# Attention's probabilities turned by VectorE and a trip through DRAM, in a mixed retention and attention layer

## The chip, the cores and the metric

One Trainium2 chip, one of its cores. A core has TensorE (PE, matmuls), VectorE (DVE), ScalarE (ACT), GpSimd (POOL) and SyncE (SP, which here only issues transfers); every engine runs its own instructions in order. Work passes between engines through semaphores, and DMA queues move data between DRAM and the on-chip memories. The metric is the device time of one execution in microseconds (us), as the median of several runs.

## What is computed

A layer of a language model on 512 tokens and 16 meta tokens, all in float32: a feed-forward part, a mixer, a second feed-forward part. The change lies in the mixer's attention (8 heads of 128), of which the reference says, cut to what matters:

```python
def hybrid_mixer(u, pos, k_top, w_in, w_ret_out, w_att_out, w_mix_out):
    proj = u @ w_in
    rq, rk, rv, rg, aq, ak, av, iq, ik, iw, g_ret, g_att = jnp.split(proj, offs, axis=-1)
    yr = retention(rope(rq), rope(rk), rv)          # four heads, normalised
    yr = (jax.nn.silu(rg) * yr) @ w_ret_out
    ya = dsa_attention(rope(aq), rope(ak), av, rope(iq), rope(ik), iw, k_top) @ w_att_out
    merged = jax.nn.sigmoid(g_ret) * yr + jax.nn.sigmoid(g_att) * ya
    return merged @ w_mix_out
```

`dsa_attention` picks 128 keys for each query by an index score, adds the meta tokens, takes the softmax over the keys that are picked and sums their values with these probabilities. (The shapes and arguments are shortened here.)

## The kernel before

**Products.** Every float32 product is made of three products of a shorter type: each operand is split into a high and a low part (`split`: a copy by ACT, L117, and a subtraction by DVE, L118), and high by high, high by low and low by high are added in PSUM (`mm3`, L157). Weights come in by `load_w` on SP's queue into `raw` (2 buffers) and are split into `whi` and `wlo` (3 buffers each); the issue of the loads is in SP's order with everything else that SP transfers.

**Order.** PE's order is that of the program text. ACT and DVE follow the text inside blocks of `manual_schedule(engines=BUSY)`; elsewhere, in attention among it, a scheduler puts their instructions in order, and SP's and POOL's as well. PSUM tiles come from two pools: `sm_tile` (one bank) and `mm_tile` (two banks, few buffers), which a projection of k (`psak`), the last rows of the scores (`psS3`), the wide gates (`psgate`, `psga`) and the weighted sum (`psao`) share.

**Attention**, about 891 to 1070 us of the span. For each head h there is a period on PE:

- `scores(q, k)`: four blocks of 128 queries (L1964; j = 2, 1, 0, 3), each over the keys up to its own block, 144, 272, 400 and 528 with the meta tokens. DVE adds the bias of the choice and finds the row's greatest, ACT takes the exponential (L1972 and on), DVE scales the rows to a sum of one (L1975). The results are `prob[j]`, tiles `pj0` to `pj3`, queries along partitions and keys along the row.
- `proj_q`, `proj_k`: projections of the next head (`psaq`, `psak`), followed by `rope_swap`: two copies by ACT (L1291, L1292), a product with the cosine on DVE (L1293), a product with the sine on POOL (L1294), the sum on DVE (L1295), and the split into `aq` and `ak`.
- `transpose_p`: the weighted sum needs keys along partitions. PE turns `prob` in 13 squares of 128 and a piece of 16 (L1988, L1990), into four PSUM tiles `psPT`, one for each 128 keys; each is split into `pth` and `ptl`. `split_rows` puts the last 16 keys into `ptail`.
- `wide_gate`: a projection for one of the gates, in an `mm_tile`, then a sigmoid on ACT (its table is loaded anew, since the exponential has another). A gate of the first kind multiplies an accumulator on POOL; one of the second (`gate_a`) is stored to DRAM, `gd`, from SP (L2010).
- `weigh_v` (`weighted`, L1536 and L1537): twelve matmuls over 512, 400, 272 and 256 queries and one small one for the meta tokens, into `psao`, which is split into `vo[..][:, h, :]`, the operand of the output projection `psat`.

The last head has no further projections; two gates stand in their place. The values come from DRAM (`vst`): `split_values` turns four heads' values at once from `vraw` into the high and low parts that lie in `vo` itself, in the place of the head's later result; the second four heads are split after head 1, and `place_tails` brings their last rows at head 3.

**Two other places.** In retention's last head (p = 3), `norm_sums(p)` puts four small matmuls in the midst of the projection `psak` (at step 4 of its 8; `between` in `mm3`), which wait for DVE's `fold`; `norm_diag(p)` at step 7 goes on from POOL's result, and `norm_all(p)` at step 2 of the next projection. Before the second feed-forward part, `rstd_folded` takes a PSUM tile `psn` (L225 to L267) and the gate's first tiles `psg` follow, which ACT's copies of the token blocks (`hTok`, L2089) still hold.

Of the kernel before, what the change touches and what calls it, by code (L numbers as in the profile page):

```python
# [18 lines left out]
P = 128  # L19
# [62 lines left out]
def kernel(ctx: ExitStack, tc: tile.TileContext, x, meta, g1, wg1, wu1, wd1, gm,  # L82
# [225 lines left out]
    fs = dpool.tile([P, 4, S], F32, name="fs")  # L308
    fk = dpool.tile([2, P, T], F32, name="fk")
    gd = dpool.tile([2 * KD, P, S], F32, name="gd")  # L310

    def gap(p, n):

# [1083 lines left out]
    if True:  # L1397
# [243 lines left out]
        def steps_of(tiles_, runs):  # L1641
            return [(*t, r, 0) for t, r in zip(tiles_, runs)]
# [196 lines left out]
            n = 4 - (h == p)  # L1839
            more += queries_keys(h) + gates[:n] + outputs(h - 1, beside_outputs(h - 1)) + gates[n:]  # L1840
        more += steps_of(tiles("gr", w_in, OFF_GR + 2 * P, 2), [proj("psgate", REAL, (), last_0), proj("psgate", REAL, (), last_1)])
        more += steps_of(tiles("ak", w_in, OFF_AK, 1), [proj("psak", None, ((4, lambda: norm_sums(p)), (7, lambda: norm_diag(p))), last_2)])
        more += steps_of(tiles("aq", w_in, OFF_AQ, 1), [proj("psaq", REAL, ((2, lambda: norm_all(p)), (4, lambda: two_normed_parts(p, 0)), (6, lambda: two_normed_parts(p, 2))), last_3)])
        more += outputs(p, lambda i: pick(2 + (i == 0)))
        more += steps_of(tiles("gr4", w_in, OFF_GR + 4 * P, 1), [proj("psgate", REAL, (), first_kq.append)])
# [56 lines left out]
    def gate_a(ps):  # L1902
# [3 lines left out]
        nc.scalar.activation(t, ps, AF.Sigmoid)  # L1906
        return t

    with pool("ao") as ao:
        vo = [ao.tile([P, AH, S], F32R, tag=f"vo{i}", name="vo") for i in range(2)]  # L1910
        ao_parts = [(vo[0][:, c, :], vo[1][:, c, :]) for c in range(AH)]
        with pool("at") as at:
            tp.update(pool=at, bufs=7)
            cos, sin = rope_tables(1, at)
            gap(at, 32)
            prob = []
            for j in range(4):
                wj = min(P * (j + 2), T)
                pj = at.tile([P, wj], F32, tag=f"pj{j}", name=f"pj{j}")
                if j < 3:  # L1920
                    nc.gpsimd.memset(pj[:, NM + P * (j + 1) :], 0.0)
                prob.append(pj)
            gap(at, 48)
            tails(at, 64)
            gap(at, 16)
            cq, ck = (Cols(w_in, o_ + P, AH - 1, step=1) for o_ in (OFF_AQ, OFF_AK))
# [52 lines left out]
            def scores(q, k):  # L1979
                for j in (2, 1, 0, 3):  # L1980
                    score(j, q, k)()

            def transpose_p():
                parts = []
                for kb in range(4):
                    ps = sm_tile("psPT")
                    for j in range(max(kb - 1, 0), 4):
                        nc.tensor.transpose(ps[:, j * P : (j + 1) * P], prob[j][:, kb * P : (kb + 1) * P], ident)  # L1988
                    if kb == 3:
                        nc.tensor.transpose(ps[:NM, 0:P], prob[3][:, 4 * P : T], ident)  # L1990
                    n = S - KQ[kb]
                    ph = at.tile([P, wide(n)], F32R, tag=f"pth{kb}", name="pth")[:, :n]
                    pl = at.tile([P, wide(n)], F32R, tag=f"ptl{kb}", name="ptl")[:, :n]
                    if kb == 3:
                        split_rows(ps[:NM, P - NM : P], tp["p"][:, :NM], "hlh")
                    split(ps[:, KQ[kb] :], ph, pl)
                    parts.append((ph, pl))
                return parts
# [14 lines left out]
            with tc.manual_schedule(engines=BUSY):  # L2013
                w = gr.next()
                k, q = rope_k(first_k, nc.vector), rope_q(first_q, nc.vector)
                t, t5 = (at.tile([P, S], F32, tag="gate", name="gate", bufs=2) for _ in range(2))
                nc.scalar.activation(t, first_gate, AF.Sigmoid)
                gate_acc(4, t)
                ps = mm_tile("psgate")[:, :S]
                mm3([(ps, REAL)], w, xs, KD)  # L2020
                w = cq.next()
                nc.scalar.activation(t5, ps, AF.Sigmoid)
                gate_acc(5, t5)
                for to_one in [score(j, q, k) for j in (2, 1, 0, 3)]:
                    to_one()
                vs = split_values(raw, [v[:, :4, :] for v in vo])
                raw = fetch_values(5, vraw())
            for h in range(AH):
                more = h + 1 < AH
                if h:  # L2030
                    scores(q, k)
                if more:
                    q, k = proj_q(w if h == 0 else None), proj_k()
                else:
                    wide_gate(sm_tile("psga"))
                    wide_gate()
                pt = transpose_p()
                wide_gate()
                weigh_v(h, pt, vs[h])
                if h == 1:  # L2040
                    with tc.manual_schedule(engines=BUSY):
                        more_vs = split_values(raw, [v[:, 4:, :] for v in vo])
                if h == 3:
                    place_tails(5)
                    vs += more_vs

        vrs.close()

        mgs = ExitStack()
        mgp = mgs.enter_context(pool("mgp", 1, side="right"))  # L2050
# [30 lines left out]
    with pool("om") as ou:  # L2081
        tp.update(pool=ou, bufs=3)
        def to_tokens(blocks):
            for c, hc in blocks:
                ps = sm_tile("psht")
                for b in range(4):
                    nc.tensor.transpose(ps[:, b * P : (b + 1) * P], hc[:, b * P : (b + 1) * P], ident)
                for b in range(4):
                    nc.scalar.activation(hTok[b][:, c * P : (c + 1) * P], ps[:, b * P : (b + 1) * P], AF.Copy)  # L2089

        cols = Cols(w_mo, 0, KD)
        pend = []
        for c in range(KD):
            hc = ou.tile([P, S], F32, tag="hc", name="hc", bufs=4)
            nc.scalar.dma_start(hc, hd[c])
            w = cols.next()
            ps = sm_tile("psmo")
            mm3([(ps, slice(0, S))], w, lambda k: mg[k], KD)
            if len(pend) == 2:
                to_tokens(pend)  # L2100
                pend = []
# [12 lines left out]

        norm = rstd_folded(ssum3, D, R3, ou, lambda: sm_tile("psn"))
        raw0 = load_w(wg2[:, 0 : 2 * P], KD, 2 * P)
        ps0 = [sm_tile("psg") for _ in range(2)]
        for i in range(2):
            w = split_w(raw0[:, :, i * P : (i + 1) * P])
            mm3([(ps0[i], RS)], w, xs, KD)  # L2120
            if i == 0:
                last_tokens()
                next(norm)
        raw0 = load_w(wu2[:, 0 : 2 * P], KD, 2 * P)
        w = split_w(raw0[:, :, :P])
        for _ in norm:
            pass
# [224 lines left out]
```

## Time and profile before

| | |
|---|---|
| median of 3 runs | 1516.9 us (1516.48 to 1517.41) |
| the profiled execution | 1516.42 us, of which the span from the first instruction to the last 1514.6 us |
| granted TensorE clock, mean | 0.998 |
| PE busy 0 to 891 us (first part, retention, choice of keys) | 888.8 us |
| PE busy 891 to 1070 us (attention) | 178.75 of 179.0 us |
| DVE, ACT busy in the same stretch | 120.5 us, 121.4 us |
| POOL busy, share of the DMA engines in the same stretch | 26.0 us, 0.35 |
| PE busy 1070 to 1130 us (output projections) | 60.0 of 60.0 us |
| PE busy 1130 to 1514 us (second feed-forward part) | 376.6 of 384.0 us |

A row of the profile gives engine, line of the kernel, operation, what is written and read, the partitions by elements of both, and the number of instructions; in the views over time the start stands first, then the duration, and in brackets how long the engine had been idle and what ended it. Matmuls overlap, so that the distance between starts tells what one costs. A group's row has busy time and mean duration, then the idle time before its instructions and its releasers. In the view of DMA issues the last number is the median time from issue to landing.

### The profile page before, as it was taken

What the parts mean: (1) busy time and instruction counts of PE and PEld (TensorE: products, weight loads), DVE (VectorE), ACT (ScalarE), POOL (GpSimd) and SP (SyncE); (2) the same over time, 40 slices, a digit from 0 to 9 for tenths busy, and PEclk for the clock granted to TensorE, in tenths of its full rate; (3) what the DMA queues carried; (4) which work ended last, traced back from release to release, by engine and by line L of the source; (5) the groups of instructions that cost most, each with busy time, mean ns of one, the idle gap of its engine ahead of it and who ended that gap; (6) DMA issues with size and microseconds to landing.
All of it is one profiled execution on the core that took longest, in us unless ns stands there. A gap on an engine that the chain in (4) does not pass through costs nothing.

```text
span 1514.6 us, 23886 instructions
## 1 busy us (share of the span) xinstructions
PE 1504.1 (99%) x9748; PEld 1368.1 (90%) x9748; DVE 1100.9 (73%) x1710; ACT 727.5 (48%) x1134; POOL 103.5 (7%) x135
## 2 busy tenths in 40 slices
PE   9999999999999999999999999999999999999997
PEld 8999999999988888888888888998888899899996
DVE  5988586786886768678888887665455888586675
ACT  5555263454354444443333357666345445264453
POOL 1000000003101120000000131110001000000000
PEclk9999999999999999999999999999999999999999
DMA  4232323226554444232323242333443223233232
GB/s 169 65 120 88 118 88 111 90 92 209 195 164 161 168 147 146 87 122 87 122 73 98 90 131 77 88 90 105 146 139 119 84 84 112 84 112 112 84 125 84
DMA packets 151741, 173.48 MB, mean 115 GB/s; under 512 B 4944, under 2 KB 123240, under 8 KB 150992
## 3 DMA queue, kind: packets, MB, share of 16 engines
q1 hardware_dynamic: 142992, 151.58, 31.6%
q0 software_dynamic: 3808, 11.38, 2.0%
q10 hardware_dynamic: 4832, 9.00, 1.6%
q8 instruction: 76, 1.25, 0.3%
q14 instruction: 33, 0.27, 0.1%
HBM read 155.94 MB, written 16.01 MB: 114 GB/s over the span
## 4 chain that ended last, share of the span: by engine, by line
PE 98%; ACT 0%; DVE 0%; issue 0%; POOL 0%; POOLq 0%; ACTq 0%
PE psqX L157 14%; PE psd L157 8%; PE psd L2187 8%; PE psqY L157 7%; PE psrg L157 6%; PE psro L157 6%; PE psvX L1180 4%; PE psqZ L157 3%; PE psrk L157 3%; PE psu L157 3%; PE psrq L157 3%; PE psaq L157 3%; PE psga L157 3%; PE psat L157 3%; PE psmo L157 3%; PE psak L157 3%
## 5 line engine op out<-in xcount | busy, mean ns | idle before, releaser
L328 ACT ACTIVATE whi<-raw 128x1024 fp32r<-128x1024 f32 (+2 forms) x184 | 169.5, 924 | 128.7 <-PE psd L157 37.6
L329 DVE TENSOR_TENSOR wlo<-raw,whi 128x1024 fp32r<-128x1024 f32 (+2 forms) x184 | 198.4, 1083 | 40.5 <-ACT whi L328 40.3
L157 PE MATMUL psqX<-th,whi 128*128 128x264 f32 (+1 forms) x432 | 122.3, 283 | 0.0
L157 PE MATMUL psqX<-tl,whi 128*128 128x264 f32 (+1 forms) x432 | 122.3, 283 | 0.0
L157 PE MATMUL psqX<-th,wlo 128*128 128x264 f32 (+1 forms) x432 | 122.2, 283 | 0.0
L118 DVE TENSOR_TENSOR wlo<-raw,whi 128x1024 fp32r<-128x1024 f32 (+1 forms) x60 | 73.6, 1227 | 52.4 <-ACT whi L117 51.5
L328 ACT ACTIVATE whi<-wsum 128x1024 fp32r<-128x1024 f32 x72 | 76.3, 1060 | 70.6 <-PE psd L2187 22.0
L117 ACT ACTIVATE whi<-raw 128x1024 fp32r<-128x1024 f32 (+1 forms) x60 | 62.3, 1043 | 85.7 <-PE psat L157 26.6
L329 DVE TENSOR_TENSOR wlo<-wsum,whi 128x1024 fp32r<-128x1024 f32 x72 | 87.8, 1221 | 12.5 <-ACT whi L328 12.5
L157 PEld LDWEIGHTS psqX<-th,whi 128*128 128x128 f32 x432 | 82.1, 190 | 0.2 <-DVE g L544 0.2
L157 PEld LDWEIGHTS psqX<-th,wlo 128*128 128x128 f32 x432 | 82.0, 190 | 0.0
L157 PEld LDWEIGHTS psqX<-tl,whi 128*128 128x128 f32 x432 | 82.0, 190 | 0.0
L157 PE MATMUL psro<-vo,whi 128*128 128x512 f32 x256 | 78.8, 389 | 0.0
L157 PE MATMUL psd<-hl,whi 128*128 128x264 f32 x352 | 71.4, 284 | 0.0
L157 PE MATMUL psd<-hh,wlo 128*128 128x264 f32 x352 | 70.8, 283 | 0.0
L157 PE MATMUL psd<-hh,whi 128*128 128x264 f32 x352 | 70.6, 282 | 0.0
L2187 PE MATMUL psd<-wlo,hh 128*128 128x512 f32 (+1 forms) x182 | 69.2, 382 | 0.0
L2187 PE MATMUL psd<-whi,hh 128*128 128x512 f32 (+1 forms) x182 | 69.2, 382 | 0.0
L2187 PE MATMUL psd<-whi,hl 128*128 128x512 f32 (+1 forms) x182 | 69.2, 382 | 0.0
L157 PEld LDWEIGHTS psro<-vo,whi 128*128 128x128 f32 x256 | 48.1, 188 | 10.1 <-DVE vo L329 0.2
L157 PEld LDWEIGHTS psd<-hh,wlo 128*128 128x128 f32 x352 | 54.5, 188 | 0.0
L157 PEld LDWEIGHTS psd<-hh,whi 128*128 128x128 f32 x352 | 54.2, 188 | 0.0
(460 smaller groups left out, 4516.2 us busy)
## 6 DMA issues: line engine op xcount, KB each, us to landing
raw<-in_ffn_w_up_dram SPq DMA_DIRECT2D x22, 1024.0 KB, 5.2
raw<-in_ffn_w_gate_dram SPq DMA_DIRECT2D x21, 1024.0 KB, 5.2
raw<-in_w_in_dram SPq DMA_DIRECT2D x18, 1024.0 KB, 5.1
raw<-in_w_in_dram SPq DMA_DIRECT2D x33, 512.0 KB, 3.7
raw<-in_ffn_w_down_dram SPq DMA_DIRECT2D x24, 512.0 KB, 4.5
w<-in_w_in_dram SPq DMA_DIRECT2D x24, 512.0 KB, 6.1
raw<-in_ffn_w_down_dram SPq DMA_DIRECT2D x12, 768.0 KB, 4.4
raw<-in_w_ret_out_dram SPq DMA_DIRECT2D x8, 1024.0 KB, 5.1
```

Of the source, the lines that this page charges most:

```text
L117: nc.scalar.activation(hi, src, AF.Copy)
L118: eng.tensor_tensor(lo, src, hi.bitcast(F32), ALU.subtract)
L157: nc.tensor.matmul(o, a[:, k, :], b[:, sl], start=first and k == 0 and i == 0, stop=last and k == nk - 1 and i == 2, skip_group_check=onto)
L328: nc.scalar.activation(hi, src, AF.Copy)
L329: return lambda: nc.vector.tensor_tensor(lo, src, hi.bitcast(F32), ALU.subtract)
L1180: nc.tensor.matmul(d[bank_][t], a, b[:, k, :], start=not onto and j + k + m == 0, stop=j + k == 3 and m == 2, skip_group_check=onto)
L2187: nc.tensor.matmul(ps, a[:, bs], m[:, j, cs], start=first and i == 0, stop=last and i == 2)
```

## The change

For heads 0 to 6 `transpose_p` and `weigh_v` are replaced by four steps; head 7 keeps the old way.

- `turn(h)`: DVE transposes `prob[j]` in squares of 32, four instructions of 13, 9, 5 and 16 squares into the tile `cross`, and one more (`crosst`) for the last 32 columns; a square keeps its place along the partitions, so the squares still have to be moved. Four transfers on POOL's queue write `cross` to DRAM (`pd`, two buffers), in rows of 512 bytes, and a small one brings the last keys to `land4`.
- `turned(h)`: four transfers on SP's queue bring `pd` back as `land0` to `land3`, 512, 512, 384 and 256 columns with keys along partitions, the queries in an order of their own.
- `turned_parts()`: the splits into `pth` and `ptl` from `land` instead of from PSUM.
- `weigh_turned(h - 1, ...)`: the weighted sum, one period later, after the next head's scores and the next projections. Its columns are 512, 512, 384, 256. In the last period it follows the scores of head 7 directly. The split of `psao` puts the queries back in order.

The values of heads 4 to 7 are split in period 0, since a sum no longer precedes them; their tails are placed at head 4. `cross` lies where `vraw` was and is set to zero on POOL. `tmp` has 4 buffers in place of 7, and the `prob` tiles are padded to whole squares.

Outside of attention: `norm_sums` of the last retention head moves from step 4 of `psak` to step 6, and the last `rstd_folded` takes its tile from `mm_tile`.

```diff
+    pd = dpool.tile([2, S, 4, P], F32, name="pd")
...
-        more += steps_of(tiles("ak", w_in, OFF_AK, 1), [proj("psak", None, ((4, lambda: norm_sums(p)), (7, lambda: norm_diag(p))), last_2)])
+        more += steps_of(tiles("ak", w_in, OFF_AK, 1), [proj("psak", None, ((6, lambda: norm_sums(p)), (7, lambda: norm_diag(p))), last_2)])
...
-            tp.update(pool=at, bufs=7)
+            tp.update(pool=at, bufs=4)
...
-                wj = min(P * (j + 2), T)
+                wj = min(P * (j + 2), T + NM)
...
+            Q0 = [0, 0, P, 2 * P]
+            land = [at.tile([P, S - q0], F32, tag=f"land{kb}", name=f"land{kb}") for kb, q0 in enumerate(Q0)]
+            land.append(at.tile([NM, NM], F32, tag="land4", name="land4"))
+            crosst = at.tile([P, 32], F32, tag="crosst", name="crosst")
...
+            def part_tiles(kb, n):
+                return [at.tile([P, S - Q0[kb]], F32R, tag=f"pt{c}{kb}", name=f"pt{c}")[:, :n] for c in "hl"]
+            def turn(h):
+                for j in (2, 1, 0, 3):
+                    m = min(-(-(NM + P * (j + 1)) // 32), 16)
+                    nc.vector.transpose(cross[:, :m, j, :], prob[j][:, : 32 * m].rearrange("p (b k) -> p b k", k=32))
+                nc.vector.transpose(crosst, prob[3][:, S : S + 32])
+                d = pd[h % 2]
+                for a in range(4):
+                    nc.gpsimd.dma_start(d.rearrange("(b i) a c -> a i b c", i=32)[a],
+                                        cross[32 * a : 32 * a + 32].rearrange("p b j c -> p b (j c)"))
+                nc.gpsimd.dma_start(land[4], crosst[96 : 96 + NM, NM:])
+            def turned(h):
+                for kb, q0 in enumerate(Q0):
+                    nc.sync.dma_start(land[kb].rearrange("p (a c) -> p a c", a=4),
+                                      pd[h % 2, kb * P : (kb + 1) * P, :, q0 // 4 :])
+            def turned_parts():
+                parts = []
+                for kb, q0 in enumerate(Q0):
+                    ph, pl = part_tiles(kb, S - q0)
+                    split(land[kb], ph, pl)
+                    parts.append((ph, pl))
+                split_rows(land[4], tp["p"][:, :NM], "hlh")
+                return parts
+            def weigh_turned(h, parts, v):
+                ps = mm_tile("psao")[:, :S]
+                for kb, q0 in enumerate(Q0):
+                    vh, vl = (part[:, kb * P : (kb + 1) * P] for part in v[:2])
+                    ph, pl = (part.rearrange("p (a c) -> p a c", a=4) for part in parts[kb])
+                    o = ps.rearrange("p (a c) -> p a c", a=4)[:, :, q0 // 4 :]
+                    if q0 == 0:
+                        (ph, pl), o = parts[kb], ps
+                    for i, (a, b) in enumerate(((vh, ph), (vh, pl), (vl, ph))):
+                        nc.tensor.matmul(o, a, b, start=kb == 0 and i == 0, stop=False)
+                nc.tensor.matmul(ps[:, KQ[4] :], v[2], tp["p"][:TR, :NM], start=False, stop=True)
+                split(*(t.rearrange(f"p ({o}) -> p a j c", a=4, j=4) for o, t in zip(("a j c", "j a c", "j a c"), (ps, *ao_parts[h]))))
...
+            pend = None
             for h in range(AH):
                 more = h + 1 < AH
                 if h:
                     scores(q, k)
                 if more:
                     q, k = proj_q(w if h == 0 else None), proj_k()
+                if pend is not None:
+                    weigh_turned(h - 1, pend, vs[h - 1])
+                if h == 0:
+                    with tc.manual_schedule(engines=BUSY):
+                        vs += split_values(raw, [v[:, 4:, :] for v in vo])
+                    vrs.close()
+                    crp = crs.enter_context(pool("cross", 1, side="right"))
+                    cross = crp.tile([P, 16, 4, 32], F32, tag="cross", name="cross")
+                    nc.gpsimd.memset(cross, 0.0)
+                if more:
+                    turn(h)
+                    wide_gate()
+                    turned(h)
+                    pend = turned_parts()
                 else:
                     wide_gate(sm_tile("psga"))
                     wide_gate()
-                pt = transpose_p()
-                wide_gate()
-                weigh_v(h, pt, vs[h])
-                if h == 1:
-                    with tc.manual_schedule(engines=BUSY):
-                        more_vs = split_values(raw, [v[:, 4:, :] for v in vo])
-                if h == 3:
+                    pt = transpose_p()
+                    wide_gate()
+                    weigh_v(h, pt, vs[h])
+                if h == 4:
                     place_tails(5)
-                    vs += more_vs
-
-        vrs.close()
+
+        crs.close()
...
-        norm = rstd_folded(ssum3, D, R3, ou, lambda: sm_tile("psn"))
+        norm = rstd_folded(ssum3, D, R3, ou, lambda: mm_tile("psn")[:, :S])
```

More of the change, by code (lines that the diff above doesn't have):

```diff
@@ L1907, in gate_a @@
         return t
+    crs = ExitStack()
     with pool("ao") as ao:
@@ L1917 @@
             for j in range(4):
-                wj = min(P * (j + 2), T)
+                wj = min(P * (j + 2), T + NM)
                 pj = at.tile([P, wj], F32, tag=f"pj{j}", name=f"pj{j}")
-                if j < 3:
-                    nc.gpsimd.memset(pj[:, NM + P * (j + 1) :], 0.0)
+                nc.gpsimd.memset(pj[:, NM + P * (j + 1) :], 0.0)
                 prob.append(pj)
-            gap(at, 48)
+            Q0 = [0, 0, P, 2 * P]
+            land = [at.tile([P, S - q0], F32, tag=f"land{kb}", name=f"land{kb}") for kb, q0 in enumerate(Q0)]
+            land.append(at.tile([NM, NM], F32, tag="land4", name="land4"))
+            crosst = at.tile([P, 32], F32, tag="crosst", name="crosst")
+            gap(at, 32)
             tails(at, 64)
@@ L1991, in transpose_p @@
                     n = S - KQ[kb]
-                    ph = at.tile([P, wide(n)], F32R, tag=f"pth{kb}", name="pth")[:, :n]
-                    pl = at.tile([P, wide(n)], F32R, tag=f"ptl{kb}", name="ptl")[:, :n]
+                    ph, pl = part_tiles(kb, n)
                     if kb == 3:
```

## The prediction

> **What bounds the kernel now.** I read the page's busy times first, then its chain of waits, then the view of what PE waited for.
>
> ```profile
> PE 1504.1 (99%) x9748; PEld 1368.1 (90%) x9748; DVE 1100.9 (73%) x1710; ACT 727.5 (48%) x1134; POOL 103.5 (7%) x135
> ```
> ```profile
> PE 98%; ACT 0%; DVE 0%; issue 0%; POOL 0%; POOLq 0%; ACTq 0%
> ```
> ```profile
> PE psg L652 <- DVE idle L620: 1.5, 1, 1.5
> PE psn L225 <- DVE fold L220: 0.8, 1, 0.8
> PE psg L157 <- ACT hTok L2089: 0.4, 1, 0.4
> PE psao L1536 <- DVE ptl L118: 0.3, 1, 0.3
> ```
>
> PE is busy 99% of the span, is 98% of the chain, and waits only 3.0 us in all. So the time is PE's own sequence: work taken off PE is gained in full, and any wait before a matmul is lost in full. One period of attention (head 1's, columns: length, then PE, PEld, DVE, ACT, POOL busy, clock, DMA share, GB/s):
>
> ```profile
> 936.26:958.60 22.34, 22.34 (x142) 20.30 (x140) 14.60 (x36) 14.76 (x28) 3.94 (x3) 1.00 0.27 72
> ```
>
> DVE has 7.7 us of room in 22.3, ACT 7.6: there is room on average, and the question is the order.
>
> **Removed from PE.** Seven heads lose their transposes.
>
> ```profile
> 927.27 1.58 PE L1988 MATMUL psPT<-ident,pj 128*128 128x128 f32 x13
> 928.69 0.27 PE L1990 MATMUL psPT<-ident,pj 128*16 128x128 f32 x1
> 928.72 0.48 PE L157 MATMUL psgate<-xh,whi 128*128 128x512 f32 x1
> 929.03 0.39 PE L157 MATMUL psgate<-xl,whi 128*128 128x512 f32 x1
> 929.26 0.39 PE L157 MATMUL psgate<-xh,wlo 128*128 128x512 f32 x1
> ```
>
> Matmuls overlap, so starts count. The gate's second starts at 929.03, and one step of such matmuls is .23 (929.26 − 929.03); without transposes the gate's first would stand at 927.27 and its second at 927.50. The gain is 1.53 a head, 7 × 1.53 = 10.7. The two mended waits are the .8 (psn) and .4 (psg) above, 1.2 if both vanish (the sums that move from step 4 to 6 leave their successor no slack that I can find, so 0 to 1.2). The .3 before psao goes with its transposes. **Gains: 12.2.**
>
> **Wider weighted sum.** Landed rows are contracted over 512, 512, 384 and 256 columns, where 512, 400, 272 and 256 were; times three products, 672 columns more.
>
> ```profile
> 934.27 0.39 PE L1536 MATMUL psao<-pth,vo 128*128 128x512 f32 x1
> ```
> ```profile
> 936.26 2.27 PE L1964 MATMUL psS<-ak,aq 128*128 128x400 f32 x15
> ```
>
> 1.99 us for 4336 columns (3 × 1440 and 16) is .459 ns a column: .31 a head, **7 × .31 = 2.2**.
>
> **Scores of head 1 wait (period 0).** The four remaining splits of `vo` are moved to period 0, two of them ahead of ak's split on DVE.
>
> ```profile
> 898.80 5.77 PE psak L157 x48
> ```
> ```profile
> 928.96 5.48 PE psgate L157 x24
> ```
> ```profile
> 906.78 1.34 POOL L1294 TENSOR_TENSOR tmp<-tmp,sin 128x528 f32<-128x528 f32 x1 [3.67 <-ACT tmp L1292]
> ```
> ```profile
> 908.15 0.71 DVE L1295 TENSOR_TENSOR tmp<-tmp 128x528 f32<-128x528 f32 x1
> ```
> ```profile
> 909.88 0.71 DVE L118 TENSOR_TENSOR ak<-tmp,ak 128x528 fp32r<-128x528 f32 x1 [0.18 <-ACT ak L117]
> ```
> ```profile
> 910.81 1.23 DVE L118 TENSOR_TENSOR vo<-vraw,vo 128x1024 fp32r<-128x1024 f32 x1
> ```
>
> PE would be through with psak at 904.57 and with the gate 5.48 later, 910.05, and then wants ak. POOL's sine product ends 908.12, DVE's sum .71 later, 908.85; then two splits of 1.23 and ak's .71 end near 911.9. **Wait 1.8** (bounds 0, the two splits elsewhere, and 2.5, both counted in full).
>
> **Weighing head 0 (period 1).** Now weigh_turned(0) stands right behind the projection of k, whose end I call E. It needs land0 and its two splits. Rows of the period above, grouped by line and shape:
>
> ```profile
> L118 DVE TENSOR_TENSOR wlo<-raw,whi 128x1024 fp32r<-128x1024 f32 x4 | 4.9, 1226 | 5.9 <-ACT whi L117 5.9
> L117 ACT ACTIVATE whi<-raw 128x1024 fp32r<-128x1024 f32 x3 | 3.2, 1063 | 3.5 <-issue 2.4 <-PE psak L157 0.7 <-PE psga L157 0.4
> L1291 ACT ACTIVATE tmp<-psak 64x528 f32<-64x528 f32 x1 | 0.6, 603 | 0.0
> ...
> L118 DVE TENSOR_TENSOR ptl<-psPT,pth 128x512 fp32r<-128x512 f32 x1 | 0.7, 690 | 0.0
> L117 ACT ACTIVATE pth<-psPT 128x512 fp32r<-128x512 f32 x1 | 0.6, 599 | 0.0
> L1906 ACT ACT_TABLE_LOAD x1 | 1.3, 1283 | 0.0
> L1383 ACT ACTIVATE gate<-psgate 128x512 f32<-128x512 f32 x1 | 0.6, 598 | 0.0
> ```
> ```profile
> 959.60 0.34 SPq L2010 DMA_DIRECT2D gd<-gate  x1
> ```
> ```profile
> sa<-gd ACTq DMA_DIRECT2D x8, 256.0 KB, 4.0
> ...
> fs<-s POOLq DMA_DIRECT2D x3, 256.0 KB, 3.2
> ...
> rqk<-fs SPq DMA_DIRECT2D x2, 256.0 KB, 5.2
> ```
>
> The trip's writes leave POOL beside the scores of head 1, two projections (11 us) before E; four issues and a landing of 3.2 (fs, of the same size) are over some 5 us before E, and if they landed that much later the stall would grow with the rest. Its reads are behind two raw loads on SP's queue, and the second load's buffer is free only when its predecessor is split; that split needs a weight buffer that PE frees at E. So: whi 1.06, wlo 1.23 (E+2.35 with a semaphore or two), the load's issue .34, land0's issue .34, landing 4.0 (reads back from DRAM: 4.0 and 5.2 measured; 4.0 taken, as eight against two), so E+7.0; pth0 .60 gives E+7.6; ptl0 .69 costs another .5, since the first product covers the rest. **Stall 8.1.** In the five middle heads the reads stand ahead of such a load in SP's queue; worked in the same manner, their last split is over 2.9 to 6.5 us before PE asks, so they cost nothing, and 1 or 2 us more of landing wouldn't show either. Independently DVE's order has ahead of ptl0, behind that wlo at E+2.3, one cosine product, two sums, the splits of aq and ak (five of .7) and head 1's transposes (1.4): even if land0 were there, about 7.1 after taking off what overlaps. So 7.1 to 9.3 (at 5.2).
>
> **Transposes on DVE.** The page has none of this kind. They cover 1408 columns a head in five instructions. The nearest one-operand pass, the softmax's scaling:
>
> ```profile
> 941.64 0.50 DVE L1975 TENSOR_SCALAR pj<-pj,stat 128x528 f32<-128x528 f32 x1
> ```
>
> That is .95 ns a column, and the two-operand sum quoted above (.71) 1.34: 1.3 to 1.9 a head. I take 1.7, nearer the slower end, since these write in a stride. They fit in the 7.7 of room; without that cover they are rival C.
>
> The Trainium skill, "VectorE: DVE Perf Modes", section "The three transpose paths", gives 311 ns for a 128x128 on VectorE, and 390 on TensorE, and its rules choose TensorE wherever PSUM will do as the destination, which speaks against this change. By its figure, 11 such tiles (1408 columns) would be an estimate of 3.4 a head, and the sum would be near rival C's; the trace's PE rows stand .11 apart in a stream, far under 390, so PE's way is also cheaper here than that figure says.
>
> **Weighing head 6 (last period).** Without a further projection, weigh_turned(6) stands right behind scores(7), 2.1 after the gate's end T.
>
> ```profile
> 914.08 2.11 PE psS L1964 x15
> ```
>
> On SP the reads stand behind the gate's store to gd, which waits for the sigmoid. ACT: whi 1.06, table 1.28, gate .60: T+2.9; store .34, land0 .34, landing 4.0: T+7.6; pth0 T+8.2, and ptl0 adds .5 as before. Less 2.1: **stall 6.6**. DVE's floor: ptl0 is issued behind the scaling of head 7's rows. In the period above, its last piece ended 5.9 behind the start of the scores (936.26; 941.64 + .50). There the sigmoid's table was loaded before the scores, here it stands ahead of the exponentials: some 1.6 later, T+7.5, and ptl0 is over at T+8.2. Less 2.1 and the .4 by which a first product runs ahead, the stall is 5.7 without any transfer. Upper end 7.8 (at 5.2).
>
> **A PSUM bank.** With psao brought forward, the gate uses psak's bank 2.3 after it (7 before). It is free after ACT's two copies (1.2) and DVE's .71, with a whi of 1.06 ahead in two periods: 3.0 less 2.3, **2 × .7 = 1.4**; 0 if ACT has the copies first.
>
> **Clock.** After PE had stood still at the start, ten matmuls took 568 ns each, the six after that 408:
>
> ```profile
> L652 PE MATMUL psg<-idle 128*128 128x512 f32 x10 | 4.0, 568 | 1.5 <-DVE idle L620 1.5
> ```
> ```profile
> L652 PE MATMUL psg<-idle 128*128 128x512 f32 x6 | 1.6, 408 | 0.0
> ```
>
> 10 × .16 = 1.6 for a cold start. In mid-kernel no wait is over .8, and none of those is followed by slower matmuls. Two stalls of 6 to 8 us lie far nearer to the cold start: **3.2** (0 to 3.2).
>
> **Sum.** 1516.4 (the profiled execution's time: span 1514.6 and 1.8 around it) − 12.2 + 2.2 + 1.8 + 8.1 + 6.6 + 1.4 + 3.2 = 1527.5. The median is .5 above that execution: **1528.0**.
>
> **Rivals.** *A, forecast*: 1528.
>
> *B, warm stalls*: the same stalls, PE at full speed behind them; 1528 − 3.2 = 1524.8. For it: no mid-kernel wait was followed by a loss; against it the cold start, the only long one. The Trainium skill, "TensorE: Matmul & The Clock Gate", section "Part 1: The HAM clock gate (the "warmup" mystery)", says that the clock halves after one idle window of about 3.4 us of a free-running counter: by it a stall over 6.8 us must meet one, a shorter one only may. No stall of before can show it.
>
> *C, DVE binds*: transposes at twice the time I take, which no row excludes. Then each period has 1.7 more on DVE ahead of the rope, and DVE reaches the product that frees psak's bank later by 1.1 in five periods (5.8 over A's 1.4), and ptl0 by 1.1: 1528 + 6.9 = 1534.9. For it: those are the instructions with no row; against it: DVE's room of 7.7, and every elementwise row at 1.34 a column or less.
>
> *D, the other side: ready in time.* If the reads of pd are issued as soon as the writes have landed (not held by the queue's loads and store), and the splits before DVE's rope and scaling work, both stalls vanish, with bank and clock: 1516.9 − 12.2 + 2.2 + 1.8 = 1508.7. It decides from where stalls, bank and clock together are under 8.2. For it: the five middle heads are so placed. Against it: in-order queues; both floors (7.1 and 5.7) together exceed 8.2, and they don't depend on a transfer.
>
> *E, one stall gone*: the other stays; 1528 − 8.1 − 1.6 = 1518.3 (period 1's gone) or 1528 − 6.6 − 1.6 = 1519.8: no difference or just slower.
>
> **How the numbers follow.** A 45%, B 24%, C 16%, E 10%, D 5%. A difference under 0.2% (3.0 us) can't be told from none. Faster takes D: .05; same, 1513.9 to 1519.9, takes most of E: .08; slower: .87. The low end, floors with warm clock and no bank wait: 1516.9 − 12.2 + 2.2 + 1.8 + 7.1 + 5.7 = 1521.5, and a little of E: 1520.5. The high end: C with half of the slower landing (5.2 for 4.0 at two stalls), 1534.9 + 1.2 = 1536.
>
> **What would show it.** In the trace of after: transposes of 416 columns near .5 us (C: near 1.0); PE waiting about 8 before the first psao of head 0, released by ACT's pth or SP's land0, and about 7 at head 6; scores of head 1 waiting near 1.8 for ak; matmuls right behind the stalls with 550 to 650 ns for 512 columns, not 390 (B); no psn or psg wait of .8 and .4. I'm wrong if the two big waits together are under 10 us, or if a wait over 1 us recurs in every period.

## The result

The changed kernel takes 1538.95 us (median of 4 runs, 1537.79 to 1541.11) against 1516.94 (4 runs, 1516.48 to 1517.41): a ratio of 1.0148, 95% interval 1.0135 to 1.0160. It is slower, as forecast, but by 22 us where 11 were forecast, and outside the range. The profiled execution took 1537.79 us, its span 1536.0.

The page of the changed kernel, busy times, the granted clock in 40 slices and the chain of waits:

```profile
PE 1505.7 (98%) x9650; PEld 1364.4 (89%) x9650; DVE 1117.2 (73%) x1745; ACT 731.0 (48%) x1134; POOL 126.8 (8%) x172
...
PEclk9999999999999999999999998999999999999999
...
PE 35%; DVE 4%; ACT 3%; issue 1%; DMA 1%; SPq 0%; POOL 0%; POOLq 0%; DVEq 0%; ACTq 0%
```

PE issues 98 matmuls fewer and is busy for longer: 1505.7 us against 1504.1. That can't be waiting, which isn't busy time; beside the 2.1 us of the wider sums it is above all the clock, which falls below 0.9 in one slice, in attention. And in attention the chain no longer stays on PE: pieces of DVE, ACT and DMA stand between PE's. (The chain was followed back only to 852 us, so its shares sum to 44%, and PE's 35% is not to be set against the 98% of before.) What PE waited for, in us, times and the longest:

```profile
PE psao L2030 <- ACT pth L117: 12.6, 2, 7.2
PE psga L157 <- DVE tmp L1295: 6.1, 5, 1.8
PE psg L654 <- DVE idle L622: 1.5, 1, 1.5
PE psS L1972 <- DVE ak L118: 1.1, 1, 1.1
PE psS L1972 <- ACT ak L117: 0.7, 1, 0.7
PE psu L157 <- ACT R L267: 0.7, 1, 0.7
PE psao L2030 <- DVE ptl L118: 0.4, 1, 0.4
PE psro L157 <- DVE vo L331: 0.2, 1, 0.2
```

The two psao waits, the scores' wait for ak and the gates' wait (psga) for the rope that frees psak's bank are all places that the prediction named. The four stretches at half clock, by windows laid around them (length, PE busy, PEld, DVE, ACT, POOL, clock, DMA share, GB/s):

```profile
913.60:917.00 3.40, 3.40 (x14) 2.91 (x13) 3.40 (x16) 3.36 (x7) 2.03 (x3) 0.50 0.56 154
930.60:940.90 10.30, 6.09 (x16) 4.91 (x17) 6.78 (x13) 4.24 (x9) 3.18 (x6) 0.50 0.83 227
1053.50:1057.00 3.50, 3.50 (x10) 2.70 (x9) 2.73 (x4) 0.64 (x1) 1.48 (x3) 0.51 0.66 154
1067.20:1070.60 3.40, 3.17 (x7) 2.19 (x8) 2.55 (x5) 1.62 (x4) 0.00 (x0) 0.50 0.91 265
```

PE is busy for 16.16 us of them, and half of that, 8.1 us, is an estimate of what full speed would have saved; by the 512-column steps, 0.43 us there and 0.23 at full speed, it is 7.5. The first stands behind two waits of 0.7 and 1.1 us with one matmul between them, the third behind a single wait of 1.8.

The transposes and the trip, grouped by shape over three periods, and the transfers' times to landing:

```profile
L1998 DVE STREAM_TRANSPOSE cross<-pj 128x512 f32<-128x512 f32 x3 | 2.1, 702 | 0.0
L1998 DVE STREAM_TRANSPOSE cross<-pj 128x416 f32<-128x416 f32 x3 | 1.8, 611 | 0.1
L1998 DVE STREAM_TRANSPOSE cross<-pj 128x288 f32<-128x288 f32 x3 | 1.4, 476 | 0.0
L1998 DVE STREAM_TRANSPOSE cross<-pj 128x160 f32<-128x160 f32 x3 | 1.0, 338 | 0.0
L1999 DVE STREAM_TRANSPOSE crosst<-pj 128x32 f32<-128x32 f32 x3 | 0.5, 166 | 0.0
```
```profile
pd<-cross POOLq DMA_DIRECT2D x28, 256.0 KB, 4.1
```
```profile
land<-pd SPq DMA_DIRECT2D x14, 256.0 KB, 3.9
```

A head's five transposes are 2.29 us, above the 1.7 that was taken and the 1.9 that bounded it; the reads land in 3.9, as taken.

Where the 21.4 us between the two profiled executions (1537.79 and 1516.42) come from, beside the terms of the prediction:

| term | predicted | measured | from |
|---|---|---|---|
| seven heads' transposes gone | -10.7 | -10.7 | no such rows outside head 7 |
| wait before psao gone | -0.3 | -0.3 | waits |
| wider weighted sum | +2.2 | +2.1 | first matmul to tail 2.26 against 1.96 |
| two mended waits | -1.2 | -0.2 | span outside attention, 1335.8 to 1335.7 (0.17 before rounding) |
| scores of head 1 | +1.8 | +1.8 | 1.1 and 0.7 |
| sum of head 0 | +8.1 | +7.6 | 7.2 and 0.4 |
| sum of head 6 | +6.6 | +5.5 | 5.46, the second of the two waits for pth |
| psak's bank | +1.4 | +6.1 | five waits |
| half clock | +3.2 | +8.1 | estimate from the windows above |
| left over | | +1.4 | ten waits, 0.14 each: without one, the next matmul starts 0.03 behind the tail's start, and the wait is counted from the tail's end, 0.17 (2.0 would be left with 7.5 for the clock) |

Attention is the stretch from the first matmul of the scores to that of the output projection: 178.77 us before (891.09 to 1069.86), 200.34 after (891.18 to 1091.52).

### The profile page after: what moved, and what is told of

Its sections match the earlier page's. It is cut to its first block, busy times and chain, and to the rows that moved or that the text cites. A ratio compares the mean times of both kernels' runs of the same rounds, so it can differ in the third digit from the quotient of the medians.

```text
span 1536.0 us, 23874 instructions
## 1 busy us (share of the span) xinstructions
PE 1505.7 (98%) x9650; PEld 1364.4 (89%) x9650; DVE 1117.2 (73%) x1745; ACT 731.0 (48%) x1134; POOL 126.8 (8%) x172
```

## The experiments

The theory from here on, called "order", is that the loss lies in where the weighted sum and the gate stand, and in what ACT, DVE and SP have ahead of the work that PE waits for. Its rival is that DVE's added work is late wherever it stands. Each run is compared with the kernel before on the same chip, 1516.5 to 1517.0 us; a time without a range or a number of runs is a single run. The changed kernel's own four runs spread over 3.3 us, so a single run shows no difference below that; there the waits in its trace are what counts.

**The mended waits alone.** On the kernel before:

```diff
-((4, lambda: norm_sums(p)), (7, lambda: norm_diag(p)))
+((6, lambda: norm_sums(p)), (7, lambda: norm_diag(p)))
-norm = rstd_folded(ssum3, D, R3, ou, lambda: sm_tile("psn"))
+norm = rstd_folded(ssum3, D, R3, ou, lambda: mm_tile("psn")[:, :S])
```

> The kernel before with the two mended waits alone. Theory 'order' (the loss comes from where the weighted sum stands, and the mended waits are nearly worth nothing, since the trace of the changed kernel shows psu waiting 0.7 for R where psg waited 0.4): 1516.5 to 1516.9 us, waits psn and psg gone, psu 0.7 there. As the prediction had it (both gone, nothing in their place): 1515.7 us.

1517.19 us (10 runs), ratio 1.0001, interval 0.9991 to 1.0011. PE's waits in it:

```profile
PE psg L652 <- DVE idle L620: 1.5, 1, 1.5
PE psu L157 <- ACT R L267: 0.7, 1, 0.7
PE psqX L157 <- DVE g L544: 0.3, 1, 0.3
PE psro L157 <- DVE vo L329: 0.2, 1, 0.2
```

The waits of 0.8 (psn) and 0.4 (psg) are gone, and 0.7, 0.3 and 0.2 stand elsewhere: PE reaches the next late thing that much earlier. No gain is measured; the interval alone would just admit 1.2 us, but the new waits sum to as much as the two that are gone.

**Only the last period mended.** On the changed kernel:

```diff
-                if pend is not None:
+                if pend is not None and more:
                     weigh_turned(h - 1, pend, vs[h - 1])
...
                     wide_gate(sm_tile("psga"))
+                    weigh_turned(h - 1, pend, vs[h - 1])
                     wide_gate()
```

> The changed kernel, with the weighted sum of head 6 moved in the last period alone, from before the two gates to between them. Theory 'order': the 5.6 us wait in front of it vanishes, and with it the half clock behind it (1.6): 1538 - 7.2 = 1531 us. Rival 'DVE' (the extra work on DVE is late wherever the sum stands): the wait moves behind the gate, 1535 us or more.

1532.54 us. Behind one gate the sum of head 6 still waits about 1.1, 0.6 for pth (the two such waits sum to 8.1, the longest is 7.5) and 0.5 for ptl, and its half clock is gone. The stall was the place, as "order" has it. This run has a second reading, on the clock. Its waits of 1.8 for gates, and windows of 3.41 us around them:

```profile
1007.43 0.50 PE L157 MATMUL psga<-xh,whi 128*128 128x512 f32 x1 [1.83 <-DVE tmp L1295]
```
```profile
1054.20 0.50 PE L157 MATMUL psga<-xh,whi 128*128 128x512 f32 x1 [1.83 <-DVE tmp L1295]
```
```profile
1005.35:1008.76 3.41, 1.58 (x10) 1.26 (x9) 2.54 (x3) 2.80 (x5) 1.98 (x3) 1.00 0.03 8
1008.76:1012.17 3.41, 3.41 (x10) 2.63 (x9) 2.34 (x4) 0.64 (x1) 2.64 (x5) 0.50 0.77 178
1053.13:1056.54 3.41, 2.34 (x10) 1.96 (x11) 2.86 (x4) 1.82 (x3) 2.99 (x4) 1.00 0.16 40
1056.54:1059.96 3.42, 3.42 (x16) 2.83 (x16) 1.33 (x3) 0.86 (x2) 0.09 (x1) 1.00 0.91 249
```

and in the changed kernel:

```profile
1007.45 0.50 PE L157 MATMUL psga<-xh,whi 128*128 128x512 f32 x1 [1.83 <-DVE tmp L1295]
```
```profile
1052.56 0.50 PE L157 MATMUL psga<-xh,whi 128*128 128x512 f32 x1 [1.83 <-DVE tmp L1295]
```
```profile
1005.78:1009.20 3.42, 1.75 (x8) 1.45 (x9) 2.62 (x4) 2.41 (x4) 2.40 (x3) 1.00 0.02 5
1009.20:1012.61 3.41, 3.41 (x17) 2.83 (x16) 1.92 (x3) 0.65 (x1) 2.20 (x5) 1.00 0.91 218
1050.15:1053.57 3.42, 1.59 (x10) 1.34 (x9) 2.23 (x3) 3.12 (x5) 1.66 (x2) 1.00 0.13 30
```

The same wait of 1.83 is followed by half clock in period 4 of the one kernel (0.50 from 1008.76) and not of the other (1.00 from 1009.20); in period 6 it is the other way about (1.00 from 1056.54 here, half clock from 1053.57 there). So the wait's length alone doesn't decide; when it falls does. The windows stand at steps of 3.41 us from the changes of the clock. In the changed kernel it changes, to the nearest 0.1 us, at 913.6, 917.0, 930.7, 940.9, 1053.6, 1057.0, 1067.2 and 1070.6, always a whole number of 3.41 us apart. At that step, one window holds the whole wait in the two cases that half clock followed, and a border between two windows cuts the wait in the two that it did not.

**Every sum behind the gate.** The same call moved behind `wide_gate()` in every period, in the last one between the gates.

```diff
-                if pend is not None:
-                    weigh_turned(h - 1, pend, vs[h - 1])
...
                     turn(h)
                     wide_gate()
+                    if pend is not None:
+                        weigh_turned(h - 1, pend, vs[h - 1])
                     turned(h)
```

> The changed kernel with every turned weighted sum behind the period's gate (in the last period between the gates). Theory 'order': no wait for psak's bank (6.8 less), none at head 6 (5.6 less), the wait at head 0 shorter by the gate's 5.5, the half-clock time behind these gone (about 4.5 to 6 less): 1539 - 22 to 24 = 1515 to 1517 us. Rival 'DVE': psao waits about 1 us in each period instead, and the sum is 1525 us or more.

1527.6 us (4 runs, 1526.9 to 1528.4), a miss for "order" by 11 us. The bank's waits are gone, but the sum of head 0 waits 3.3 still and that of head 6 some 2.9, and the scores now wait for ak, 4.2 us in all: the scheduler made another order of ACT and DVE from the new text. The time lies where the rival put it, but not by its mechanism: no sum of heads 1 to 5 waits for pth or ptl.

**The bank alone.** The changed kernel with the gates in another PSUM pool, nothing moved:

```diff
                     turn(h)
-                    wide_gate()
+                    wide_gate(sm_tile("psga") if pend is not None and gr.at == gr.n else None)
```

> The changed kernel, with the gates of periods 3 to 7 (those in psga) in a tile of the small PSUM pool, so that they need not wait for psak's bank; nothing is moved. Theory 'order': the five psga waits (6.1 us, with 0.7 of pipeline) and the 1.7 us of half clock behind the one at 1052 vanish: 1538 - 8.5 = 1529.5 us, or up to 4 more if the projection of q then waits for the gate's sigmoid in the small pool. Rival 'DVE': the late work shows up in front of the next scores instead, 1536 us or more.

1528.29 us, 9.5 less than the changed kernel's profiled execution. PE's waits in attention:

```profile
PE psao L2030 <- ACT pth L117: 11.5, 2, 7.2
...
PE psS L1972 <- DVE ak L118: 1.1, 1, 1.1
PE psS L1972 <- ACT ak L117: 0.9, 1, 0.9
PE psao L2030 <- DVE ptl L118: 0.4, 1, 0.4
```

No psga wait is left, and nothing came in its place: in the middle periods DVE's work as such fits. The 9.5 us are not the bank's alone: its waits were 6.1, the stall of head 6 is 1.1 shorter in this run (4.3), and psu's 0.7 isn't there. Half clock lasts 20.5 us in both, since the stretch in period 6 is gone and the one behind head 6's stall is 6.8 long instead of 3.4.

**Few squares.** The transposes cut to one column of squares each, which leaves out part of the computation: the probabilities that come back are not the softmax's.

```diff
-nc.vector.transpose(cross[:, :m, j, :], prob[j][:, : 32 * m].rearrange("p (b k) -> p b k", k=32))
+nc.vector.transpose(cross[:, :1, j, :], prob[j][:, :32].rearrange("p (b k) -> p b k", k=32))
```

> The changed kernel with the transposes of DVE cut to one column of squares each (32 columns for 416, 288, 160 and 512), so that the probabilities that come back are not the softmax's: this part of the computation is left out. It takes 1.7 us a head off DVE. Theory 'order' (what frees psak's bank late is where ACT and DVE have these instructions in their order, and the gate's own place): the stalls at heads 0 and 6 and most of the bank's waits stay, 1534 to 1538 us. Rival 'DVE' (the transposes' time is what is late): the five psga waits vanish and ptl comes earlier, 1527 us or less.

1538.56 us, as slow as the changed kernel, 0.6 above what "order" gave and far from the rival's 1527.

```profile
PE psao L2030 <- ACT pth L117: 12.8, 2, 7.3
PE psga L157 <- DVE tmp L1295: 6.0, 5, 2.5
```

The transposes take 6.6 us for the seven heads where they took 16.1, and the two kinds of wait sum to what they did. The single gates' waits did change, from between 0.8 and 1.8 to between 0.5 and 2.5, so the order was another one too, and the run can't say what sets each. But time off DVE by itself brought nothing. With these two runs the rival, as it was put for the changed kernel, has fallen.

**Seven heads, both mends.** The gates in the small pool as above, and the sum of head 6 behind both gates of the last period.

```diff
-                if pend is not None:
+                if pend is not None and more:
...
                     wide_gate(sm_tile("psga"))
                     wide_gate()
+                    weigh_turned(h - 1, pend, vs[h - 1])
                     pt = transpose_p()
```

> The changed kernel with the gates of periods 3 to 7 in the small PSUM pool and the weighted sum of head 6 behind both gates of the last period. All that is left of the loss is then in the first two periods: scores of head 1 (2 us and 2 us of half clock) and the sum of head 0 (7.6 and 2 to 3). Theory 'order': 1528.3 - 5.6 - 2 = 1520.5 us.

1520.54 us (8 runs, 1518.21 to 1521.81), ratio 1.0023, interval 1.0013 to 1.0034. As expected: what is left is the first two periods, where head 0's sum still waits 7.3 and 0.3 and the scores of head 1 wait 0.8 and 1.1.

**Six heads.** On the version before, head 0 turned and weighed by PE in the old way:

```diff
+                if h == 0:
+                    pt = transpose_p()
+                    wide_gate()
+                    weigh_v(h, pt, vs[h])
...
-                if more:
+                elif more:
                     turn(h)
```

> As the run before, and head 0 is turned and weighed by PE in the old way, with the splits of the other four values behind it: six heads are turned by DVE and DRAM. Theory 'order': no wait is left, 1516.9 - 6 x 1.53 + 6 x .31 = 1509.6 us, up to 1511 with a small wait or two; faster than both kernels. Rival (the work on DVE, ACT and in the queues can't be covered in a period whatever the order): 1515 us or more.

1511.24 us (5 runs, 1510.59 to 1512.24), ratio 0.9965, interval 0.9952 to 0.9977: faster than both kernels. One wait of 1.5 and 0.9 for ak is left, before the scores of head 2. The rival, 1515 us or more, has fallen here too.

**The stores on ACT's queue.** On the changed kernel:

```diff
-nc.sync.dma_start(gd[KD + ga.at - 1], t)
+nc.scalar.dma_start(gd[KD + ga.at - 1], t)
```

> The changed kernel with the gates' stores to gd issued from ACT right behind the sigmoid, so that the reads of pd don't stand behind them on SP's queue. Theory 'landing' (in periods 4 and 6 psak's bank comes free 1.8 us late because the chain store, read of pd, split on ACT and DVE, rope of q, rope of k runs in that order): the two psga waits of 1.83 fall under 1.0, the three others stay, and head 6 gains nothing much (its floor on DVE is 5.7): 1535 to 1537 us. Rival 'bank alone' (the place of the gate behind psao sets it, whatever lands): all five waits as before, 1538 us.

1541.18 us, and the psga waits are 8.5 in all, the longest 2.6. Both expectations missed: the scheduler put one more split of weights ahead of ACT's copies. The stall of head 6, which was to gain nothing much, fell from 5.5 to 3.6 (3.4 and 0.2), with the reads of `pd` out of the store's way. What makes the bank late is read from period 6 of the changed kernel, first ACT's rows, then DVE's, in order of time:

```profile
1042.55 1.06 ACT L117 ACTIVATE whi<-raw 128x1024 fp32r<-128x1024 f32 x1 [0.43 <-ACT pj L1978]
1043.56 1.38 ACT L117 ACTIVATE pth<-land 128x512 fp32r<-128x512 f32 x2
...
1049.89 0.63 ACT L117 ACTIVATE aq<-tmp 128x512 fp32r<-128x512 f32 x1 [2.85 <-DVE tmp L1297]
1050.54 0.60 ACT L1293 ACTIVATE tmp<-psak 64x528 f32<-64x528 f32 x1
```
```profile
1045.27 3.18 DVE L118 TENSOR_TENSOR ptl<-land,pth 128x512 fp32r<-128x512 f32 x4
1048.38 0.68 DVE L1295 TENSOR_TENSOR tmp<-psaq,cos 128x512 f32<-128x512 f32 x1
...
1051.80 0.71 DVE L1295 TENSOR_TENSOR tmp<-psak,cos 128x528 f32<-128x528 f32 x1 [0.55 <-ACT tmp L1294]
```

The four splits of the landed probabilities stand ahead of q's cosine on DVE; ACT's copy into aq waits for q's sum (2.85), and the copies out of psak stand behind it on ACT; k's cosine frees the bank at 1052.5, and the gate starts at 1052.56. That is an order in which a projection of k that ended at 1048.3 gets its bank read out 4 us later. The landing has a part in it that isn't settled: the changed kernel's chain of waits goes through a read of `pd` in periods 2 and 6 (4.0 and 4.7 us), and not in 4. Whether an earlier landing would help by itself stays open, since this run changed the order as well.

**The values' splits later.** Six heads, the four splits behind the gate of period 1 (the diff is shortened):

```diff
                 elif more:
+                    if h == 1:
+                        wide_gate()
+                        with tc.manual_schedule(engines=BUSY):
+                            vs += split_values(raw, [v[:, 4:, :] for v in vo])
...
+                        turn(h)
```

> As the version with six heads turned, and the four splits of the later values stand behind the gate of period 1 instead of ahead of it. Theory 'order': the wait of 2.4 us for ak in front of the scores of head 2, and the half clock behind it (1.7), vanish if the turn of head 1, now 5 us later on DVE, still lands in time: 1511.2 - 4.3 = 1507 us. Rival: the turn of head 1 comes too late, and a wait of 1 to 3 us in front of its weighted sum takes the place: 1509 to 1512 us.

1510.98 us (5 runs), ratio 0.9962, where "order" gave 1507: the wait of 1.5 and 0.9 is where it was, so the splits weren't its cause in this version. The rival's wait before the weighted sum didn't come either, though the time lies in its range. ACT's rows there:

```profile
933.21 1.06 ACT L117 ACTIVATE whi<-raw 128x1024 fp32r<-128x1024 f32 x1 [3.18 <-PE psgate L157]
934.17 0.63 ACT L117 ACTIVATE ak<-tmp 128x528 fp32r<-128x528 f32 x1
```

ACT stood 3.2 us before a split that needed the gate's end, with ak's copy behind it; the sum on DVE that this copy needs had been over at 932.2.

**Pinned.** On that version, in period 1, k's projection, rope and gate in a block with the program's order:

```diff
+                    with tc.manual_schedule(engines=BUSY):
+                        w = ck.next()
+                        parts, ps = halves(mm_tile("psak"))
+                        mm3(parts, w, xs, KD)
+                        i_gate, w = KD - gr.n + gr.at, gr.next()
+                        k = rope_k(ps)
+                        ps = mm_tile("psgate")[:, :S]
+                        mm3([(ps, REAL)], w, xs, KD)
```

> As the run before, with the projection of k and the gate of period 1 in a block whose order is the program's, so that ACT's copy into ak stands ahead of the next weights' split, which waits for the gate's end. Theory 'order' (the 2.4 us wait in front of the scores of head 2 is ACT's order, not the splits of the values): that wait vanishes, 1511.0 - 2.4 = 1508.6 us. Rival (DVE's or POOL's work is late whatever ACT's order): the wait stays or moves, 1510.5 us or more.

1510.81 us (5 runs), where the wait's going would have given 1508.6 and the rival 1510.5 or more: nothing changed, the split of the next weights belongs to code outside of the block and was still put ahead. So the next run has it inside, as `w = cq.next()` at the end of the block.

> As the run before, in which the scheduler still put the split of the weights of the next projection of q ahead of ACT's copy into ak. Here that split stands in the pinned block too, behind the copy. Theory 'order': the waits of 1.5 and 0.9 in front of the scores of head 2 vanish and no wait over 0.3 is left in attention, 1510.8 - 2.4 = 1508.4 us. Rival (DVE, POOL or the queues are late whatever ACT's order): 1510.5 us or more.

1510.99 us (5 runs), where "order" gave 1508.4 and the rival 1510.5 or more. The wait in period 1 is gone, and one of 1.6 and 0.3 stands before the scores of head 3, where the scheduler still chose. The last run has the block in periods 1 to 6, with the weighted sum's matmuls in it.

> As the run before, with the same pinned order in every period from 1 to 6 (ACT's copy into ak, and the copy of psao, ahead of the next weights' splits). In the run before, the wait of 1.6 and 0.3 turned up in the next period, where the scheduler still chose. Theory 'order': no wait over 0.3 in attention, 1511.0 - 2.0 = 1509 us. Rival (the sum of the work on ACT, DVE and POOL in a period is the limit): a wait of 1 us or more stays somewhere, 1510.5 us or more.

1510.39 us (5 runs, 1509.76 to 1510.65), ratio 0.9956, interval 0.9943 to 0.9970. PE's waits from 925 to 1075 us:

```profile
PE psaq L157 <- DVE stat L1975: 1.7, 1, 1.7
PE psao L2030 <- DVE ptl L118: 0.2, 1, 0.2
```

Again the wait found another place, behind the scores of head 3. There two splits of weights, 2.4 us from 955.1, stand on DVE ahead of its pass over these scores, and PE's next projection starts at 958.1. "Order" gave 1509 and no wait over 0.3; its rival, that the sum of the work on ACT, DVE and POOL is the limit, gave a wait of 1 us or more, which came, and 1510.5 or more, which the time misses by 0.1. So the last two us are not settled: each run shows what stood ahead of the late work, but none shows an order without such a wait. This version has the lowest median, 6.6 us under the kernel before; the five versions with six heads can't be told from one another.

## Why the prediction was wrong

**Right.** PE's sequence sets the time, and the gain of the transposes, the wider sum, the stall of head 0 and its releaser (ACT's pth) came out as worked. The scores' wait has the size that was worked out, 1.8, but part of it by luck: 0.7 of it is for ACT's copy into ak, behind two of ACT's copies for `vo` that the sum didn't have, and which had themselves waited for the values' landing. Head 6 was 1.1 too long: its first split was over 7.6 behind the scores' start, not 8.2, and the second came in time for its product. Nor was 5.7 a floor: with the stores on ACT's queue, and with that run's order on DVE, it waited 3.6. The prediction's own signs of being wrong, big waits under 10 us or a wait over 1 us in every period, did not come: the waits were 13.0, and two of the five gates' waits were over 1.

**The step on the PSUM bank** failed. It counted a wait where a weight split stands ahead of ACT's two copies, in two periods, and said that it is free at 3.0 behind the projection. In those two (periods 3 and 5) the waits were 0.8 each, as worked. But the step took the copies out of psak to be next on ACT elsewhere, and in the other three periods (2, 4 and 6) ACT had aq's copy ahead, which hung on q's rope, which stood behind the splits of what had landed. There the waits were 0.9, 1.8 and 1.8. The prediction had found that the landed rows are split in time for their own use, and from that took them to cost nothing; it didn't ask what they are in front of. The run with gates in the other pool, which has none of these waits, shows that they were the bank's, 6.1 us where 1.4 were predicted.

**The step on the clock** failed more: 3.2 predicted, 7.5 to 8.1 by the windows. It charged a cold start to the two long stalls alone, by the row of ten slow matmuls, and from waits under 0.8 took it that short ones are free. The waits in between, of 1.8, were not asked about; two of them brought half clock. And the stall of head 0 left PE at half speed for its whole restart, 6.1 busy us in place of some 3. The rival without any clock loss (B) fell by the rows at 0.50.

**The mended waits** were taken as 1.2, and no gain was measured: PE met the next late releaser.

**The transposes** cost 2.29 a head, over the bound. The price was taken by the column, and there are five instructions: between 160 and 512 columns the time grows by 1.0 ns a column (338 to 702 ns), which leaves by estimate 0.17 us for each instruction, whatever its columns. The 311 and 390 ns that the prediction quotes stand in the Trainium skill, "VectorE: DVE Perf Modes", section "The three transpose paths", for 128x128 in bf16, while these tiles are float32. The 3.4 a head that it worked out from the 311 was too long here. Rival C rested on the transposes, and its sum, 1534.9, lies nearest to the time (by its own 1.1 in five periods it would be 1534.6, since they sum to 5.5 and not to 5.8), but the mechanism is not C's: cut transposes leave the sum of the waits as it was. C's waits in five periods were there, in three of them from the splits that stand in front of the rope. Rival D needed both stalls to vanish; the six-head versions reach that by taking head 0 out and the last sum behind the gates.

## What to carry to other kernels

When work leaves the bounding engine for others, ask of each new instruction not only whether it is ready in time itself but what stands behind it in its engine's order; a split that is early for its own reader can be late for the next PSUM bank. Price a wait of a couple of microseconds on PE at up to twice its length, for the slow clock behind it (1.8 us of wait brought up to 1.7 more). Ask of the first and the last member of a pipelined loop what work there is to cover them, and leave one in the old way where there is none. Here a loss of 22 us became one of 4 by giving the gates another pool and putting the last sum behind the gates, and then a gain of 5 by leaving head 0 in the old way.

## What the hardware showed

PE fell to half clock after waits of 1.8 us, not only of 5 or 7, in stretches of 3.4 us or three times as long (10.2). The Trainium skill, "TensorE: Matmul & The Clock Gate", section "Part 1: The HAM clock gate (the "warmup" mystery)", has the clock go by a free-running window of 3.4 us and halve after an idle one. The stretches agree with that length, and that the same wait of 1.83 us throttled in one place and not in another agrees with windows that run by themselves: it throttled where one window held all of it. That a whole window must be idle doesn't agree: the wait that ended at 1052.56 was 1.83, about half a window, and half clock began about 1053.6. The 512-column steps there were 0.43 us instead of 0.23.

How idle a window must be is not settled. In the changed kernel and in the run with only the last period mended, windows in which PE was busy for 1.58, 1.59 and 1.71 us were followed by half clock, and those with 1.75 and 2.34 were not. But the window from 1060.39 to 1063.81 of the changed kernel, in which the stall of head 6 began, was busy for only 1.56, and the clock fell one window later. The wait of 1.5 and 0.9 in the first version with six heads fell into a window that was busy for 1.41 and brought half clock (from 936.6 to 940.0); in the pinned version a border cut it, the windows were busy for 2.17 and 2.31, and the clock stayed.

A DVE transpose of 32-square blocks took 611 ns for 416 columns and 702 for 512, 1.4 to 1.5 ns a column; the two-operand splits of 512 columns in the same periods took 678, so that the two passes cost nearly the same.
